# A two-layer hybrid decoder on one NeuronCore: late squares of the FFN norm, three attention stages, alternating GLA heads, 72 decay rows, another ending and a shorter warm-up

## The chip, the core and the metric

The kernel runs on one core of a Trainium2 chip. The metric is the device time of one execution, in microseconds (us); lower is better. The engines are TensorE (PE, with its weight loads shown apart as PEld), VectorE (DVE), ScalarE (ACT), GpSimd (POOL) and SyncE (SP, which issues most transfers). Each takes its instructions in the order in which they are in its queue.

## What is computed

Two layers over 512 positions of 1024 features, in float32. Each layer normalises x, makes one input projection, and gives its columns to four mixers: FoX (softmax attention with a cumulative log forget gate), GLA (gated linear attention in chunks of 64), MLA (attention over low-rank latents with a rotary part) and Mamba-2 SSD (with a convolution). Their outputs go through one output projection, and then come a second norm and a SwiGLU FFN. Cut to the frame:

```python
for l in range(DEPTH):
    h = rmsnorm(x, norm1[l])
    (fq, fk, fv, ff, gq, gk, gv, gr, gg, mcq, mckv, mkr, sz, sxbc, sdt) = split_cols(h @ w_in[l], IN_SPLITS)
    y_a = fox_mixer(fq, fk, fv, ff, fox_f_bias[l])
    y_b = gla_mixer(gq, gk, gv, gr, gg, gla_gate_w2[l], gla_gate_b[l], gla_out_norm[l])
    y_c = mla_mixer(mcq, mckv, mkr, positions, mla_q_norm[l], mla_w_uq[l], mla_kv_norm[l], mla_w_ukv[l])
    y_d = mamba2_mixer(sz, sxbc, sdt, ...)
    x = x + jnp.concatenate([y_a, y_b, y_c, y_d], axis=-1) @ w_out[l]
    h2 = rmsnorm(x, norm2[l])
    x = x + (jax.nn.silu(h2 @ w_gate[l]) * (h2 @ w_up[l])) @ w_down[l]
return rmsnorm(x, final_norm)
```

The four attention heads of FoX and of MLA are 64 wide; each query block has 128 positions and sees the keys up to its own block.

## The kernel before

x is held transposed: eight chunks `xT[0..7]` of 128 features by 512 positions. Each float32 operand of a large product is split in a high half (fp32r, made on ACT) and a low half (the rest, made on DVE), for weights (`wh`, `wl`, L293 and L294) and for activations. A product (`prod`, L315 to L317) is three matmuls for each chunk of 128 features: high by high, high by the weight's low half, and the activation's low half by high. Weights come by DMA from SP two ahead of their use, and only ACT and DVE stand between the transfer and the product.

The order of the instructions of PE, DVE and ACT is planned when the program is built, from the order of the code and the dependences; `tc.issue_after(x)` holds what follows in the code behind instruction x. The mixers are generators: `R.step()`, called after each product of the projections, takes the running ones a step on, so that their small pieces of work lie between the products.

The FFN norm is `norm2`. After each product of the last part of the output projection (tile `om`) the sum with x is made on DVE (L1072), `chunk` makes the chunk's high and low half with the norm's gain (`n_0h` on ACT, L363; `n_0l` on DVE, L364), and `square` squares the chunk on ACT (L371, L374) and adds it to the accumulator `n_0acc` on POOL, the last one on DVE (L375). The factor of the root is applied later, to the products. `first_two` (L396 to L407) computes the first columns of gate and up, `g` and `u`, over the first KC-1 = 7 of the 8 chunks, g then u, and then over the last chunk, and behind that sums the accumulator over the features (`n_0ms`, L407). In layer 1 the same tiles are called `n_1h`, `n_1l` and so on.

The decays of the SSD heads are a tile `jrr` of 40 rows by 512: rows 0 to 7 hold the high halves, rows 32 to 39 the low halves. The matmul `pb` (L526) picks one head's row with the matrix `sel` and spreads it over 128 partitions; there are four per layer. GLA adds the part from earlier chunks in groups of 14 matmuls (L671), two groups per layer, each for two heads: 7 chunks of one head, then 7 of the other. One matmul of float32 leaves two records in the trace. The two heads read other rows (32 each) and write other partitions (64 each) of one accumulator.

Attention (L682 to L735) works on 8 blocks (two pairs of heads, four query blocks). `front` makes the scores of one head (`sf` or `sm`, L692), mask and maximum on DVE, exponential and scaling on ACT. `back` turns the weights around on PE (`ptf` or `ptm`, L709), copies them on ACT (`atf` or `atm`, L711) and multiplies by v on PE (`fo` or `mo`, L714). The loop calls `front` for block j and then `back` for block j-1.

The end is `last_part`: the last products add to xT, and `xg` and the squares follow. Its last two chunks, 6 and 7, are computed in halves of the positions by `part(i, half, ...)`. `finish(half)` transposes `xg` (L777), sums the squares over partitions (`fms`, L805), scales and writes `foo` to the output (L814). In the second half all 16 transposes stand in `finish`. At the start, WARM matmuls of ones (`pps`, L195) run while x and the first weights come.

Of the kernel before, what the change touches and what calls it, by code (L numbers as in the profile page):

```python
# [17 lines left out]
ALU = mybir.AluOpType  # L18
# [22 lines left out]
RATE_F, RATE_M, RATE_S, RATE_G = 2, 2, 1, 2  # L41
WARM = 14
ROPE_AT = 3
# [92 lines left out]
def trunk(tc, I, out, shapes, depth=2):  # L136
# [7 lines left out]
    with ExitStack() as es:  # L144
# [74 lines left out]

        sel = cp.tile([40, 4, P], F32R, name="sel")  # L220

        def selectors():
            for half in range(2):
                V.tensor_copy(gmask[blk(half, 64)], tri[blk(half, 64), blk(half, 64)])
            for h in range(4):
                V.tensor_tensor(sel[:, h, :], ident[0:40, 4 + h:5 + h].broadcast_to((40, P)),
                                ident[0:40, 36 + h:37 + h].broadcast_to((40, P)), op=ALU.add)

# [123 lines left out]
        class Norm:  # L352


            def __init__(self, g0, name):
                self.g0, self.name, self.act = g0, name, []
# [39 lines left out]
            def first_two(self, pa_, pb_, split=KC - 1, with_col=True):  # L396

                wa, wb = W.get(), W.get()
                for ks in (range(split), range(split, KC)):
                    for ps, w in ((pa_, wa), (pb_, wb)):  # L400
                        last = prod(ps, w, self.act, ks=ks)
                with tc.issue_after(last.ins):
                    if with_col:
                        self.columns()
                        return self.spread()
                    ps = ps_mix(f"{self.name}ms")
                    PE.matmul(ps, lhsT=ones, rhs=self.acc, start=True, stop=True)  # L407
                    return rsqrt(ps, D, "f", self.name, sp.tile([P, T], F32, tag="rn", name=f"{self.name}r"))
# [13 lines left out]
        def joint_gates(l, sm, res):  # L422
# [161 lines left out]
        def gla(l, q, k, v, rg, Gc, res):  # L584
# [58 lines left out]
            for pr in range(2):  # L643
# [39 lines left out]
        def attention(l, nm, terms, v, res):  # L683
# [17 lines left out]

            def back(p, qb, ss, o):
                for k0 in range(0, qb + 1, 2):
# [7 lines left out]
                    S.copy(t[:, :n], pt[:, :n])  # L711
                    for kb in kbs:
                        for hh in range(2):
                            PE.matmul(o[blk(hh, 64), blk(qb)], lhsT=v[kb // 2][:, blk(4 * (kb % 2) + 2 * p + hh, 64)],  # L714
                                      rhs=t[:, blk(2 * (kb - k0) + hh)], start=kb == 0, stop=kb == qb)

            blocks = [(p, qb) for p in range(2) for qb in range(NB)]
            o, held = None, []
            for j in range(len(blocks) + 1):
                if j < len(blocks):  # L720
                    p, qb = blocks[j]
                    while len(terms) <= 2 * p + 1:
                        yield
                    held.append([])
                    for hh in range(2):
                        if hh:
                            yield
                        held[-1].append(front(2 * p + hh, qb))
                if j:
                    p, qb = blocks[j - 1]  # L730
                    if qb == 0:
                        o = ps_acc(f"{nm}o{l}_{p}")
                    back(p, qb, held.pop(0), o)
                    if qb == NB - 1:
                        res.append(mix_operand(o, f"{nm}{l}_{p}"))  # L735
                yield
# [23 lines left out]
        def last_part(us):  # L760


            acc, xg, banks = tmp("g", "nfacc"), [], {}

            def feature(m, ps, t):
                V.tensor_tensor(xT[m][:, t], xT[m][:, t], ps[:, t], op=ALU.add)
                V.tensor_scalar(xg[m][:, t], xT[m][:, t], col(104 + m), None, op0=ALU.mult)
                sq = tmp("f", f"nfq{m}") if m else acc
# [29 lines left out]
            def finish(half):  # L798
                bs = range(2 * half, 2 * half + 2)
                for m in range(KC) if half else (6, 7):  # L800
                    for b in bs:
                        turn(b, m, ps_proj if m >= 4 else ps_mix)
                ps = ps_mix(f"fms{half}")
                for b in bs:
                    PE.matmul(ps[:, b % 2:b % 2 + 1], lhsT=acc[:, blk(b)], rhs=onec, start=True, stop=True)  # L805
                rc = rsqrt_col(ps[:, 0:2], f"nf{half}", 2)
                for h in range(2):
                    for b in bs:
# [3 lines left out]
                        else:  # L812
                            S.activation(o, banks[b, h], AF.Copy, scale=rc[:, b % 2:b % 2 + 1])
                        nc.sync.dma_start(out[0, blk(b), blk(h, T)], o)  # L814

# [72 lines left out]
        for l in range(depth):  # L888
# [80 lines left out]
            for c in range(2):  # L969
                hold = {}  # L970
                for nm, scale, one, row in (("k", 1.0, -1.0, 66), ("q", -0.125, 1.0, 64)):
                    ps = ps_proj(f"f{nm}p{l}_{c}")
                    prod(ps, W.get(), act)
                    for hh in range(2):
# [9 lines left out]
                        G.memset(b.bitcast(F32)[64:68], one)  # L984
                        nc.gpsimd.dma_start(b[row:row + 2], rr[h:h + 33:32])
                        hold[nm, hh] = a, b
# [76 lines left out]
            for nm, ops in (("g", mix_g), ("m", mix_m)):  # L1063
                if nm == "m":
                    R.drain(g_m)
                for i in range(2):
                    w = W.get()
                    for c in range(4):
# [71 lines left out]
```

## Time and profile before

| | before |
|---|---|
| median of 3 runs | 1269.92 us (1268.7 to 1270.27) |
| profiled execution | 1269.87 us |
| its span, first to last instruction | 1268.1 us |
| mean granted TensorE clock | 0.994 |
| PE busy | 1248.9 us, 98% of the span |
| DVE, ACT, POOL busy | 694.0, 533.5, 179.1 us |

The profile is of one execution, and the span leaves out 1.77 us of its time. Busy time is summed over the instructions of an engine; a matmul's shown length is longer than its step, as matmuls are pipelined, so steps are read from start to start. A granted clock of 1.00 is 2.4 GHz for TensorE and 0.50 is 1.2 GHz.

### The profile page before, as it was taken

Reading aid. Unit: us, or ns where it says so; the run is one execution under the profiler, and the core shown is the slowest. Engines: PE = TensorE matmul, PEld = TensorE weight load, DVE = VectorE, ACT = ScalarE, POOL = GpSimd, SP = SyncE. Lnnn points to the kernel's source line nnn. Section 1 sums busy time; section 2 is a strip of 40 time slices with the busy share of each in tenths; the row PEclk is TensorE's granted clock in tenths of the full one; section 3 lists DMA queues with packets and bytes.
Section 4 is the critical chain, followed back from the end, with each engine's and each line's share of the span. In section 5 each row is a group of like instructions: output and inputs, shape, how many; then the busy total and the mean of one; then the engine's idle time right before and its main releaser. Section 6 shows DMA issues by size and latency. Waiting matters only on the chain.

```text
span 1268.1 us, 16210 instructions
## 1 busy us (share of the span) xinstructions
PE 1248.9 (98%) x6402; PEld 1014.5 (80%) x6402; DVE 694.0 (55%) x1132; ACT 533.5 (42%) x882; POOL 179.1 (14%) x163
## 2 busy tenths in 40 slices
PE   9999999989999999999999999999899999999997
PEld 7887787768888888888888877777788888888886
DVE  7877697565443333344557677966644334433444
ACT  6557765543222222223444577565422222212232
POOL 0103210031100110111301122000211011101111
PEclk9999999989999999999999999999999999999999
DMA  6222121113333333332323221212233223333232
GB/s 206 89 84 67 58 68 45 47 60 116 90 95 99 100 94 91 103 96 89 110 83 101 84 67 43 67 34 67 68 116 97 89 96 100 89 109 98 88 89 76
DMA packets 32907, 109.99 MB, mean 87 GB/s; under 512 B 4096, under 2 KB 4256, under 8 KB 32832
## 3 DMA queue, kind: packets, MB, share of 16 engines
q1 hardware_dynamic: 31968, 108.54, 27.7%
q8 instruction: 50, 0.82, 0.3%
q10 hardware_dynamic: 288, 0.34, 0.1%
q14 instruction: 25, 0.20, 0.0%
q0 software_dynamic: 576, 0.08, 0.0%
HBM read 106.79 MB, written 2.10 MB: 86 GB/s over the span
## 4 chain that ended last, share of the span: by engine, by line
PE 92%; DVE 5%; ACT 2%; DMA 1%; issue 0%; POOL 0%; SPq 0%; DVEq 0%
PE u L315 6%; PE u L316 6%; PE u L317 6%; PE g L317 6%; PE g L315 6%; PE g L316 6%; PE d L315 5%; PE d L316 5%; PE d L317 5%; PE ft L317 3%; PE ft L316 3%; PE ft L315 3%; PE sm L692 1%; PE oa L316 1%; PE oa L315 1%; PE oa L317 1%
## 5 line engine op out<-in xcount | busy, mean ns | idle before, releaser
L293 ACT CAST wh<-wr 128x1024 fp32r<-128x1024 f32 (+2 forms) x206 | 210.3, 1023 | 567.1 <-issue 342.5
L294 DVE TENSOR_TENSOR wl<-wr,wh 128x1024 fp32r<-128x1024 f32 (+2 forms) x206 | 249.9, 1213 | 73.2 <-ACT wh L293 73.0
L315 PE MATMUL d<-uh,wh 128*128 128x512 f32 x296 | 115.1, 389 | 0.0
L316 PE MATMUL d<-uh,wl 128*128 128x512 f32 x296 | 115.1, 389 | 0.0
L317 PE MATMUL d<-ul,wh 128*128 128x512 f32 x296 | 115.1, 389 | 0.0
L1097 DVE TENSOR_TENSOR ft<-u,fs 128x512 f32<-128x512 f32 x44 | 30.4, 692 | 132.7 <-PE u L317 127.1
L1111 DVE TENSOR_TENSOR xT<-xT,d 128x512 f32<-128x512 f32 x40 | 27.5, 688 | 104.6 <-PE d L317 104.6
L1094 POOL TENSOR_TENSOR fs<-fs,n_0r 128x512 f32<-128x512 f32 x22 | 38.3, 1744 | 280.4 <-ACT fs L1093 280.4
L1094 POOL TENSOR_TENSOR fs<-fs,n_1r 128x512 f32<-128x512 f32 x22 | 38.3, 1745 | 279.3 <-ACT fs L1093 279.3
L317 PE MATMUL g<-n_1l,wh 128*128 128x512 f32 x176 | 69.0, 392 | 2.3 <-DVE n_1l L364 2.3
L317 PE MATMUL g<-n_0l,wh 128*128 128x512 f32 x176 | 69.0, 392 | 2.3 <-DVE n_0l L364 2.3
L315 PE MATMUL g<-n_0h,wh 128*128 128x512 f32 x176 | 69.0, 392 | 0.8 <-ACT n_0h L363 0.8
L315 PE MATMUL g<-n_1h,wh 128*128 128x512 f32 x176 | 69.0, 392 | 0.8 <-ACT n_1h L363 0.8
L315 PE MATMUL u<-n_0h,wh 128*128 128x512 f32 x176 | 69.5, 395 | 0.0
L316 PE MATMUL u<-n_0h,wl 128*128 128x512 f32 x176 | 69.4, 394 | 0.0
L317 PE MATMUL u<-n_0l,wh 128*128 128x512 f32 x176 | 69.4, 394 | 0.0
L315 PE MATMUL u<-n_1h,wh 128*128 128x512 f32 x176 | 69.0, 392 | 0.0
L317 PE MATMUL u<-n_1l,wh 128*128 128x512 f32 x176 | 69.0, 392 | 0.0
L316 PE MATMUL u<-n_1h,wl 128*128 128x512 f32 x176 | 68.9, 392 | 0.0
L316 PE MATMUL g<-n_0h,wl 128*128 128x512 f32 x176 | 68.5, 389 | 0.0
L316 PE MATMUL g<-n_1h,wl 128*128 128x512 f32 x176 | 68.5, 389 | 0.0
L317 PEld LDWEIGHTS d<-ul,wh 128*128 128x128 f32 x296 | 55.6, 188 | 11.6
(614 smaller groups left out, 2823.5 us busy)
## 6 DMA issues: line engine op xcount, KB each, us to landing
wr<-in_weights_dram SPq DMA_DIRECT2D x168, 512.0 KB, 3.5
wr<-in_weights_dram SPq DMA_DIRECT2D x32, 448.0 KB, 3.2
xT<-in_x_dram SPq DMA_DIRECT2D x8, 256.0 KB, 6.8
out_dram<-foo SPq DMA_DIRECT2D x8, 256.0 KB, 2.4
wr<-in_weights_dram SPq DMA_DIRECT2D x6, 256.0 KB, 4.1
posi<-in_positions_dram ACTq DMA_DIRECT2D x1, 256.0 KB, 3.0
fkb<-jrr POOLq DMA_DIRECT2D x8, 4.0 KB, 2.7
fqb<-jrr POOLq DMA_DIRECT2D x8, 4.0 KB, 1.7
```

Source lines behind the costliest of these rows:

```text
L293: S.copy(h[:, c], raw[:, c])
L294: V.tensor_tensor(lo[:, c], raw[:, c], h.bitcast(F32)[:, c], op=ALU.subtract)
L315: PE.matmul(ps, lhsT=wh[:, k, c0:c0 + P], rhs=ah, start=k == 0, stop=False)
L316: PE.matmul(ps, lhsT=wl[:, k, c0:c0 + P], rhs=ah, start=False, stop=False)
L317: last = PE.matmul(ps, lhsT=wh[:, k, c0:c0 + P], rhs=al, start=False, stop=k == n - 1)
L692: PE.matmul(ps[:, :n], lhsT=q[:d, blk(qb)], rhs=k[:d, :n], start=i == 0, stop=i == len(terms[h]) - 1)
L1094: G.tensor_tensor(s, s, r, op=ALU.mult)
L1097: V.tensor_tensor(t, pu, s, op=ALU.mult)
L1111: V.tensor_tensor(xT[m], xT[m], ps, op=ALU.add)
```

## The change

1. `norm2`: no `square` between the chunks; `first_two` puts all squares and their sum behind the last chunk's halves, all adds on DVE, and its split is 6 and 2 chunks instead of 7 and 1.
2. `jrr` and `sel` have 72 rows; the low halves lie in rows 64 to 71.
3. GLA's loop over chunks is outside, that over the two heads inside.
4. Attention: `back` is split in `turn` (transposes and copies) and `values` (products by v). In step j come the values of block j-2, the scores of block j, and the transposes of block j-1.
5. Ending: the squares of chunk 7 are not added on DVE, but summed over partitions by matmuls of their own into the same place; eight transposes of the second half stand ahead of that half's last products; the second half's other transposes take buffers of another pool; the output's last piece is issued by ACT.
6. WARM is 11 instead of 14.

The core of the diff:

```diff
-WARM = 14
+WARM = 11
...
-        sel = cp.tile([40, 4, P], F32R, name="sel")
+        sel = cp.tile([72, 4, P], F32R, name="sel")
...
-                V.scalar_tensor_tensor(al, src, g, ah.bitcast(F32), op0=ALU.mult, op1=ALU.subtract)
+                low = V.scalar_tensor_tensor(al, src, g, ah.bitcast(F32), op0=ALU.mult, op1=ALU.subtract)
                 self.act.append((ah, al))
-                return high
+                self.last = high, low
...
                 for ks in (range(split), range(split, KC)):
                     for ps, w in ((pa_, wa), (pb_, wb)):
                         last = prod(ps, w, self.act, ks=ks)
+                if self.acc is None:
+                    high, low = self.last
+                    with tc.issue_after(high.ins), tc.issue_after(low.ins):
+                        for k in range(KC):
+                            self.square(k, V)
...
-            rr = sp.tile([40, T], F32R, tag="jrr", name=f"jrr{l}")
+            rr = sp.tile([72, T], F32R, tag="jrr", name=f"jrr{l}")
             G.memset(rr.bitcast(F32), 0.0)
             V.tensor_copy(rr[0:8], rows)
-            V.tensor_tensor(rr[32:40], rows, rr.bitcast(F32)[0:8], op=ALU.subtract)
+            V.tensor_tensor(rr[64:72], rows, rr.bitcast(F32)[0:8], op=ALU.subtract)
...
-                for hh in range(2):
-                    h = 2 * pr + hh
-                    for c in range(1, 8):
+                for c in range(1, 8):
+                    for hh in range(2):
+                        h = 2 * pr + hh
                         PE.matmul(o[blk(hh, 64), blk(c, 64)], lhsT=st[c][blk(h, 32), :],
...
-            for j in range(len(blocks) + 1):
+            for j in range(len(blocks) + 2):
+                if j < len(blocks):
+                    while len(terms) <= 2 * blocks[j][0] + 1:
+                        yield
+                if j >= 2:
+                    p, qb = blocks[j - 2]
+                    if qb == 0:
+                        o = ps_acc(f"{nm}o{l}_{p}")
+                    values(p, qb, turned.pop(0), o)
+                    if qb == NB - 1:
+                        res.append(mix_operand(o, f"{nm}{l}_{p}"))
                 if j < len(blocks):
...
+                    held.append([front(2 * p, qb)])
+                    yield
+                    held[-1].append(front(2 * p + 1, qb))
+                if 0 < j <= len(blocks):
+                    turned.append(turn(*blocks[j - 1], held.pop(0)))
                 yield
...
-                if m:
+                if m == KC - 1:
+                    end[t.start] = sq
+                elif m:
...
-                for m in range(KC) if half else (6, 7):
+                for m in range(4, KC) if half else (6, 7):
...
                 for b in bs:
-                    PE.matmul(ps[:, b % 2:b % 2 + 1], lhsT=acc[:, blk(b)], rhs=onec, start=True, stop=True)
+                    for sq in (acc, end[256 * half]):
+                        PE.matmul(ps[:, b % 2:b % 2 + 1], lhsT=sq[:, blk(b)], rhs=onec, start=sq is acc,
+                                  stop=sq is not acc)
...
-            part(0, 1, range(SECOND_HALF, n))
+            last = part(0, 1, range(SECOND_HALF, n))
+            with tc.issue_after(last.ins):
+                for m in range(4):
+                    for b in (2, 3):
+                        turn(b, m, ps_mix)
             part(1, 1, range(n))
...
                         if nm == "m":
                             norm2.chunk(m)
-                            norm2.square(m)
...
-                        r = norm2.first_two(pg, pu, with_col=False)
+                        r = norm2.first_two(pg, pu, KC - 2, with_col=False)
```

How the change moves instructions, at three places. A row is a line of the code, the operation, and the tiles that it writes and reads.

The first is DVE at the end of the output projection of layer 0, where `xT` is the residual add, `wl` a weight's low half, `n_0l` a chunk's low half. Before:

```order
L364 SCALAR_TENSOR_TENSOR n_0l_2727<-xT_86,pcv,n_0h_2726 128x512
L1072 TENSOR_TENSOR xT_88<-xT_88,om_5_2754 128x512
L294 TENSOR_TENSOR wl_2736<-wr_2733,wh_2735 128x1024
L364 SCALAR_TENSOR_TENSOR n_0l_2748<-xT_87,pcv,n_0h_2747 128x512
L364 SCALAR_TENSOR_TENSOR n_0l_2763<-xT_88,pcv,n_0h_2762 128x512
L1072 TENSOR_TENSOR xT_89<-xT_89,om_6_2769 128x512
L1072 TENSOR_TENSOR xT_90<-xT_90,om_7_2784 128x512
L294 TENSOR_TENSOR wl_2804<-wr_2801,wh_2803 128x1024
L364 SCALAR_TENSOR_TENSOR n_0l_2778<-xT_89,pcv,n_0h_2777 128x512
L364 SCALAR_TENSOR_TENSOR n_0l_2793<-xT_90,pcv,n_0h_2792 128x512
L375 TENSOR_TENSOR n_0acc<-n_0acc,n_0q_2796 128x512
```

Now:

```order
L1094 TENSOR_TENSOR xT_88<-xT_88,om_5_2737 128x512
L1094 TENSOR_TENSOR xT_89<-xT_89,om_6_2749 128x512
L364 SCALAR_TENSOR_TENSOR n_0l_2734<-xT_87,pcv,n_0h_2733 128x512
L364 SCALAR_TENSOR_TENSOR n_0l_2746<-xT_88,pcv,n_0h_2745 128x512
L1094 TENSOR_TENSOR xT_90<-xT_90,om_7_2761 128x512
L364 SCALAR_TENSOR_TENSOR n_0l_2758<-xT_89,pcv,n_0h_2757 128x512
L294 TENSOR_TENSOR wl_2778<-wr_2775,wh_2777 128x1024
L364 SCALAR_TENSOR_TENSOR n_0l_2770<-xT_90,pcv,n_0h_2769 128x512
L375 TENSOR_TENSOR n_0acc<-n_0acc,n_0q_2837 128x512
L375 TENSOR_TENSOR n_0acc<-n_0acc,n_0q_2840 128x512
L375 TENSOR_TENSOR n_0acc<-n_0acc,n_0q_2843 128x512
L375 TENSOR_TENSOR n_0acc<-n_0acc,n_0q_2846 128x512
```

Six more adds into `n_0acc` stand on DVE behind the last low half (seven in all), and none stands on POOL; the last weight split ahead of the FFN has moved back by one low half.

The second is PE in FoX of layer 0, around the transposes of block (1, 2). Before, with `gvp` a product of the input projection and `fo` the values:

```order
L709 MATMUL ptf_1_2_0_1744<-ident,asf_2_2_1623 128x128
L709 MATMUL ptf_1_2_0_1744<-ident,asf_3_2_1632 128x128
L709 MATMUL ptf_1_2_0_1744<-ident,asf_2_2_1623 128x128
L709 MATMUL ptf_1_2_0_1744<-ident,asf_3_2_1632 128x128
L709 MATMUL ptf_1_2_2_1755<-ident,asf_2_2_1623 128x128
L709 MATMUL ptf_1_2_2_1755<-ident,asf_3_2_1632 128x128
L324 MATMUL gvp_2_1772<-wh_1521,n_0h_154 128x256
L325 MATMUL gvp_2_1772<-wl_1522,n_0h_154 128x256
L326 MATMUL gvp_2_1772<-wh_1521,n_0l_155 128x256
L324 MATMUL gvp_2_1772<-wh_1521,n_0h_165 128x256
L714 MATMUL fo_1_1569<-atf_1_2_0_1749,fv_0_895 64x128 x4
L714 MATMUL fo_1_1569<-atf_1_2_2_1758,fv_1_896 64x128 x2
```

Now:

```order
L326 MATMUL gvp_1_1693<-wh_1584,n_0l_234 128x256
L726 MATMUL fo_1_1614<-atf_1_1_0_1640,fv_0_892 64x128 x4
L698 MATMUL sf_2_3_1723<-fka_2_1074,fqa_2_1160 128x512
L698 MATMUL sf_2_3_1723<-fkb_2_1075,fqb_2_1161 128x512
L698 MATMUL sf_3_3_1732<-fka_3_1083,fqa_3_1169 128x512
L698 MATMUL sf_3_3_1732<-fkb_3_1084,fqb_3_1170 128x512
L717 MATMUL ptf_1_2_0_1741<-ident,asf_2_2_1620 128x128
L717 MATMUL ptf_1_2_0_1741<-ident,asf_3_2_1629 128x128
L717 MATMUL ptf_1_2_0_1741<-ident,asf_2_2_1620 128x128
L717 MATMUL ptf_1_2_0_1741<-ident,asf_3_2_1629 128x128
L717 MATMUL ptf_1_2_2_1748<-ident,asf_2_2_1620 128x128
L717 MATMUL ptf_1_2_2_1748<-ident,asf_3_2_1629 128x128
```

The values behind these transposes, four products after them before, come a step later; those of the block ahead stand in front of the scores `sf`.

The third is PE at the end, behind the last product. Before (8 more transposes ahead of these rows):

```order
L777 MATMUL fo_1_10168<-ident,xg_9946 128x128
L777 MATMUL fo_1_10166<-ident,xg_9984 128x128
L777 MATMUL fo_1_10168<-ident,xg_9984 128x128
L777 MATMUL fo_1_10166<-ident,xg_10020 128x128
L777 MATMUL fo_1_10168<-ident,xg_10020 128x128
L777 MATMUL fo_1_10166<-ident,xg_10022 128x128
L777 MATMUL fo_1_10168<-ident,xg_10022 128x128
L805 MATMUL fms_10176<-ones,nfacc 128x1 x2
```

Now, behind the last product, and then behind the last product of chunk 6's second half:

```order
L793 MATMUL fo_1_10163<-ident,xg_9943 128x128
L793 MATMUL fo_1_10165<-ident,xg_9943 128x128
L793 MATMUL fo_1_10163<-ident,xg_9981 128x128
L793 MATMUL fo_1_10165<-ident,xg_9981 128x128
L793 MATMUL fo_1_10163<-ident,xg_10017 128x128
L793 MATMUL fo_1_10165<-ident,xg_10017 128x128
L822 MATMUL fms_10173<-ones,nfacc 128x1
L793 MATMUL fo_1_10163<-ident,xg_10019 128x128
L793 MATMUL fo_1_10165<-ident,xg_10019 128x128
L822 MATMUL fms_10173<-ones,nfq_256_10161 128x1
L822 MATMUL fms_10173<-ones,nfacc 128x1
L822 MATMUL fms_10173<-ones,nfq_256_10161 128x1
```

```order
L316 MATMUL dl_10018<-uh_21_9793,wl_9948 128x256
L317 MATMUL dl_10018<-ul_21_9794,wh_9947 128x256
L793 MATMUL fo_0_10128<-ident,xg_9799 128x128
L793 MATMUL fo_0_10130<-ident,xg_9799 128x128
L793 MATMUL fo_0_10128<-ident,xg_9835 128x128
L793 MATMUL fo_0_10130<-ident,xg_9835 128x128
L793 MATMUL fo_0_10128<-ident,xg_9871 128x128
```

Eight transposes have moved ahead of the last 21 products, and the sum over partitions is made by four matmuls, two of which read the squares of chunk 7, `nfq_256`.

## Rows read from the trace of the kernel before

**Rows 1.** The page: the start of the chain that ended last, shares of the span.
```profile
PE 92%; DVE 5%; ACT 2%; DMA 1%; issue 0%; POOL 0%; SPq 0%; DVEq 0%
```

**Rows 2.** Two stretches: us, busy of PE, PEld, DVE, ACT, POOL; granted clock; DMA.
```profile
256.00:268.00 12.00, 12.00 (x54) 9.94 (x53) 11.59 (x14) 9.57 (x15) 6.83 (x5) 1.00 0.17 50
...
276.00:280.00 4.00, 4.00 (x11) 3.10 (x10) 0.00 (x0) 0.00 (x0) 0.00 (x0) 0.50 0.00 0
```

**Rows 3.** Timeline, PE, FFN start of both layers: start, us, what [idle before].
```profile
265.74 0.39 PE L315 MATMUL g<-n_0h,wh 128*128 128x512 f32 x1
...
269.36 0.39 PE L316 MATMUL g<-n_0h,wl 128*128 128x512 f32 x1
...
274.16 0.79 PE L317 MATMUL g<-n_0l,wh 128*128 128x512 f32 x1 [1.92 <-DVE n_0l L364]
...
283.34 1.02 PE L407 MATMUL n_0ms<-n_0acc,ones 128*128 128x512 f32 x2
...
889.47 0.39 PE L315 MATMUL g<-n_1h,wh 128*128 128x512 f32 x1
...
905.92 1.02 PE L407 MATMUL n_1ms<-n_1acc,ones 128*128 128x512 f32 x2
```

**Rows 4.** Tiles n_0l, n_0q (ns min/median/max) and timeline, DVE and POOL.
```profile
L364 DVE SCALAR_TENSOR_TENSOR n_0l<-xT,pcv,n_0h x16: 736/752/1779, 5.3 to 274.0; 128x512 fp32r<-128x512 f32 x16
...
266.63 3.48 DVE L364 SCALAR_TENSOR_TENSOR n_0l<-xT,pcv,n_0h 128x512 fp32r<-128x512 f32 x2
...
260.86 8.69 POOL L375 TENSOR_TENSOR n_0acc<-n_0acc,n_0q 128x512 f32<-128x512 f32 x5 [44.79 <-ACT n_0q L374]
...
L374 ACT ACTIVATE n_0q<-xT x14: 613/618/625, 16.5 to 272.5; 128x512 f32<-128x512 f32 x14
L375 DVE TENSOR_TENSOR n_0acc<-n_0acc,n_0q x8: 676/692/695, 17.4 to 274.7; 128x512 f32<-128x512 f32 x8
```

**Rows 5.** Timeline, PE, around one decay product and one 68-row score product.
```profile
98.42 0.28 PE L325 MATMUL fvp<-wl,n_0h 128*128 128x256 f32 x1
98.54 0.28 PE L326 MATMUL fvp<-wh,n_0l 128*128 128x256 f32 x1
98.75 0.50 PE L526 MATMUL pb<-jrr,sel 40*128 40x512 f32 x1
99.18 0.50 PE L315 MATMUL fkp<-n_0h,wh 128*128 128x512 f32 x1
99.52 0.40 PE L316 MATMUL fkp<-n_0h,wl 128*128 128x512 f32 x1
...
132.97 0.40 PE L692 MATMUL sf<-fkb,fqb 68*128 68x512 f32 x1
133.20 0.40 PE L692 MATMUL sf<-fka,fqa 128*128 128x512 f32 x1
```

**Rows 6.** PE, line 671: timeline of one group, then two stretches of it (records in brackets).
```profile
194.11 1.66 PE L671 MATMUL go<-gq,gst 32*64 32x64 f32 x28
...
195.00:195.30 0.30, 0.30 (x12) 1.00 0.00 0
...
195.30:195.60 0.30, 0.30 (x9) 1.00 0.00 0
```

**Rows 7.** Waits, PE: total us, times, longest, attention values.
```profile
PE fo L714 <- ACT atf L711: 2.6, 6, 0.9
```

**Rows 8.** Timeline, PE, start; and the chain that ended last in the same stretch.
```profile
1.14 6.13 PE L195 MATMUL pps<-ones 128*128 128x128 f32 x28 [1.14 <-DVE ones L187]
...
3.62 6.75 DMA xT<-in_x_dram
```

**Rows 9.** Timeline, end: PE, DVE and ACT after the last product.
```profile
1258.78 1.91 PE L777 MATMUL fo<-ident,xg 128*128 128x128 f32 x16
...
1259.49 0.42 ACT L769 ACTIVATE nfq<-xT 128x256 f32<-128x256 f32 x1 [1.39 <-DVE xT L766]
...
1260.53 0.50 PE L805 MATMUL fms<-ones,nfacc 128*128 128x1 f32 x4
```

More of the change, by code (lines that the diff above doesn't have):

```diff
@@ L225, in selectors @@
             for h in range(4):
-                V.tensor_tensor(sel[:, h, :], ident[0:40, 4 + h:5 + h].broadcast_to((40, P)),
-                                ident[0:40, 36 + h:37 + h].broadcast_to((40, P)), op=ALU.add)
+                V.tensor_tensor(sel[:, h, :], ident[0:72, 4 + h:5 + h].broadcast_to((72, P)),
+                                ident[0:72, 68 + h:69 + h].broadcast_to((72, P)), op=ALU.add)
         gsgn = cp.tile([P, 8], F32, name="gsgn")
@@ L355, in __init__ @@
             def __init__(self, g0, name):
-                self.g0, self.name, self.act = g0, name, []
+                self.g0, self.name, self.act, self.acc = g0, name, [], None
             def chunk(self, k, src=None):
@@ L700, in front, with turn @@
                 return s
-            def back(p, qb, ss, o):
+            def turn(p, qb, ss):
+                ts = []
                 for k0 in range(0, qb + 1, 2):
@@ L711, in back @@
                     S.copy(t[:, :n], pt[:, :n])
[L712 to L715, printed above, removed]
-            blocks = [(p, qb) for p in range(2) for qb in range(NB)]
-            o, held = None, []
-            for j in range(len(blocks) + 1):
+                    ts.append(t)
@@ new lines, in turn, with values @@
+                return ts
+            def values(p, qb, ts, o):
+                for kb in range(qb + 1):
+                    for hh in range(2):
+                        PE.matmul(o[blk(hh, 64), blk(qb)], lhsT=v[kb // 2][:, blk(4 * (kb % 2) + 2 * p + hh, 64)],
+                                  rhs=ts[kb // 2][:, blk(2 * (kb % 2) + hh)], start=kb == 0, stop=kb == qb)
+            blocks = [(p, qb) for p in range(2) for qb in range(NB)]
+            o, held, turned = None, [], []
+            for j in range(len(blocks) + 2):
[9 more added lines that the diff above has]
+                        res.append(mix_operand(o, f"{nm}{l}_{p}"))
@@ L720, in attention @@
                 if j < len(blocks):
                     p, qb = blocks[j]
[L722 to L735, printed above, removed]
+                    held.append([front(2 * p, qb)])
@@ L760, in last_part @@
         def last_part(us):
-            acc, xg, banks = tmp("g", "nfacc"), [], {}
+            acc, xg, banks, end = tmp("g", "nfacc"), [], {}, {}
             def feature(m, ps, t):
@@ L767, in feature @@
                 V.tensor_scalar(xg[m][:, t], xT[m][:, t], col(104 + m), None, op0=ALU.mult)
-                sq = tmp("f", f"nfq{m}") if m else acc
+                sq = tmp("f", f"nfq{m}_{t.start}") if m else acc
                 S.activation(sq[:, t], xT[m][:, t], AF.Square)
-                if m:
+                if m == KC - 1:
+                    end[t.start] = sq
+                elif m:
                     (G if m < KC - 2 else V).tensor_tensor(acc[:, t], acc[:, t], sq[:, t], op=ALU.add)
@@ L799, in finish @@
                 bs = range(2 * half, 2 * half + 2)
-                for m in range(KC) if half else (6, 7):
+                for m in range(4, KC) if half else (6, 7):
                     for b in bs:
-                        turn(b, m, ps_proj if m >= 4 else ps_mix)
+                        turn(b, m, ps_acc)
                 ps = ps_mix(f"fms{half}")
                 for b in bs:
-                    PE.matmul(ps[:, b % 2:b % 2 + 1], lhsT=acc[:, blk(b)], rhs=onec, start=True, stop=True)
+                    for sq in (acc, end[256 * half]):
+                        PE.matmul(ps[:, b % 2:b % 2 + 1], lhsT=sq[:, blk(b)], rhs=onec, start=sq is acc,
+                                  stop=sq is not acc)
                 rc = rsqrt_col(ps[:, 0:2], f"nf{half}", 2)
@@ L813, in finish @@
                             S.activation(o, banks[b, h], AF.Copy, scale=rc[:, b % 2:b % 2 + 1])
-                        nc.sync.dma_start(out[0, blk(b), blk(h, T)], o)
+                        (nc.scalar if (half, h, b) == (1, 1, 2) else nc.sync).dma_start(out[0, blk(b), blk(h, T)], o)
             n = len(us)
@@ L984, in trunk @@
                         G.memset(b.bitcast(F32)[64:68], one)
-                        nc.gpsimd.dma_start(b[row:row + 2], rr[h:h + 33:32])
+                        nc.gpsimd.dma_start(b[row:row + 2], rr[h:h + 65:64])
                         hold[nm, hh] = a, b
```

## The prediction

> **What bounds the kernel.** The first view is the page's chain of waits, followed back from the last instruction: 92% of it is TensorE (PE), 5% VectorE (DVE), 2% ScalarE (ACT) [rows 1]. So time is gained only where PE idles, runs at the lower clock, or spends more than a product's normal pitch on an instruction. The second view, a table of stretches, finds the large loss. From 256 to 268 us DVE is busy 11.59 of 12 us, and from 276 to 280 us PE is busy all the time at a granted clock of 0.50, its 1.2 GHz level [rows 2]. The timeline of that place shows the order of events: the FFN's products run evenly from 265.74, one waits 1.92 us for the low half `n_0l` at 274.16, and after these waits the clock is low until about 280 [rows 2, 3]. I then looked at single instructions whose pitch (start to next start) is above that of their kind, at PE's waits, and at both ends of the program [rows 5 to 9].
>
> The sum is made against the profiled execution, 1269.87 us (span 1268.1 and 1.77 around it), which is 0.05 below the median of the runs.
>
> **FFN norm.** The first two hidden columns are 48 products. Undisturbed they stand (269.36 - 265.74) / 16 = 0.226 us apart, 10.85 us in all. In layer 0 they take 283.34 - 265.74 = 17.60 us, in layer 1 905.92 - 889.47 = 16.45 [rows 3]. The losses are 6.75 and 5.60, together 12.35 us; they are both the waits and the products at the lower clock. What is late is DVE, which takes its instructions in order: a low half takes 0.75 us as a rule, but the two from 266.63 on take 3.48 together, while POOL is inside its five adds of squares from 260.86 to 269.55, 1.74 us each [rows 4]. The change takes all six POOL adds out, puts the squares and their sum behind the last low half on ACT and DVE, and holds back two chunks rather than one in both columns. The last low half starts at 274.0 now and would end near 274.8. The pair at 266.63 alone is 2.0 us over two at 0.75; the others behind chunk 1 are stretched too, up to 1.78 [rows 4], and I take 4.2 us for all, which puts the end at 270.6. With the new order it is the 42nd product that needs it, at 265.74 + 41 x 0.226 = 275.0; even with the 2.0 us of the pair alone (272.8) it is in time. So nothing waits there, and without a wait I expect no low clock. ACT's eight squares at 0.62 are 5.0 us behind the high halves, to about 275.5, and the last add of 0.69 ends near 276.2 [rows 4]; PE is through its 48 products at 265.74 + 10.85 = 276.6. The sum is ready 0.4 us before it is needed. That is narrow, but a miss of some tenths costs those tenths only. Term: **-12.3**. The other end: if the DVE adds take POOL's 1.74 us, seven of them after 271.2 end at 283.4, which is when the sum of squares is read now, and the gain is nothing.
>
> **72 decay rows.** A decay product on 40 rows is 99.18 - 98.75 = 0.43 us, where a score product of the same 512 columns on 68 rows is 0.23. The product before it has a pitch of 0.21 instead of 0.12, the one after it 0.34 instead of 0.23 [rows 5]. So its tile size, unlike its neighbours', costs 0.20 + 0.09 + 0.11 = 0.40. There are eight. With 72 rows it is a tile of the neighbours' size: 8 x 0.40 = **-3.1**, rounding down. Setting 72 rows to zero or copying the decay rows to partition 64 costs no more per instruction, as the length per row is unchanged; at the other end nothing is gained.
>
> **GLA heads alternate.** A group of 28 records lasts 1.66 us, 0.058 per record, the two heads one after the other [rows 6]. Around the place where the first head ends and the second begins, 12 records fall into 0.30 us; later, in the second head alone, 9 do [rows 6]. The records of two heads, which use other rows and other columns of the array, start in pairs there. With the heads alternating all can pair: 14 x 0.058 and about 0.14 for the two edges are 0.95, a saving of 0.64, and 4 x 0.64 = **-2.5**. The other end is 0. A rule speaks against this term: the Trainium skill (TensorEngine Tiling (Array Packing), Gotcha 1: PSUM Pressure) says that different row tiles cannot access one PSUM bank at the same time. Both heads write one bank, so by that rule the term would be 0. The 12 records against 9 in the same bank speak against the rule.
>
> **Attention in three stages.** A block's scores (front), the transposes of its weights (turn) and its product with v (values) were two pieces, the values right behind the transposes, or a few products behind. Now the values stand one step later, ahead of the next scores. PE waited 2.6 us in six places for the copy `atf` that the values read [rows 7]; a step of products now lies between, and I take all of it. Further, values and scores stand side by side, so products change their kind less often; counted over PE's order that is 15 switches fewer each way. A switch shows 0.09 to 0.11 around a decay product [rows 5]; 15 x 0.1 less what two split groups in the out-projection cost is 1.0. Term: **-3.6**, between -6 (if the shorter waits of weight loads count as well) and +1.6 (the six waits stay, six more of their mean, 0.43, come at the new place, and only the 1.0 is gained).
>
> **Shorter warm-up.** 28 records in 6.13 us become 22, so the first product could start some 1.3 us earlier. But behind it the chain of waits goes back to the transfer of x, from 3.62 to 10.37 [rows 8]. Cover is that transfer; **0**, from -0.3 to +1.5 (if the products before it ran at the lower level of the clock, half the pace, for 3 us more).
>
> **The end.** Two instructions per half become four sums over partitions, and each is two records of 0.12 (four in 0.50) [rows 9]. In the first half these four more records lie on the path: +0.45. Eight of the last sixteen transposes, (1260.53 - 1258.78) / 16 = 0.109 each [rows 9], go ahead of the last part's products. They do not vanish; they move those products by 0.87, and one more change of kind adds 0.09. Behind the last product there were 16 transposes and 4 records, 2.2 us. Now 6 transposes run while ACT's last square comes, 1259.49 + 0.42 - 1258.78 = 1.13 after the transposes began [rows 9]; two transposes and six records behind it end some 1.85 after, 0.35 sooner. The last output's issue from ACT beside SP may give 0.1. Sum 0.45 + 0.96 - 0.35 - 0.1: **+1.0**, between -1.3 (the eight transposes and DVE's dropped add of 0.42 count in full) and +1.4.
>
> **Sum.** -12.3 - 3.1 - 2.5 - 3.6 + 0 + 1.0 = -20.5, so 1269.87 - 20.5 = **1249.4 us**.
>
> **Rivals.**
> 1. *The sum of squares is late.* ACT's eight squares, DVE's seven adds and PE's reading of them lie within 0.4 us. If they come 3 us late in each layer, PE idles before `n_0ms`, and the clock may fall behind that wait as it does now. Half of the FFN term goes: 1255.5. For it: DVE is full up to the last low half. Against it: POOL no longer works beside it.
> 2. *GLA gains nothing*, because records of two heads that write the same bank follow each other as those of one head do: 1249.4 + 2.5 = 1251.9. Against it stand the 12 records in 0.30 us. This is how the kernel would go by the Trainium skill's page TensorEngine Tiling (Array Packing), Gotcha 1.
> 3. *The squares do not do what they are moved for.* If low halves are slow for another reason than POOL's adds, the waits and the low clock stay: 1249.4 + 12.3 = 1261.7. Against it: the lows are at 0.75 wherever POOL is idle.
> 4. *Slower: the values block the scores.* PE takes its instructions in order, and the values now stand in front of the next scores in each of 32 steps (two layers, two attentions, eight blocks). If ACT's copy is late there, the scores wait as well, then DVE and ACT behind them, and the next copy is late again. The longest present wait of this kind is 0.9 us [rows 7]; at every step it would be 28.8 us, and 1278. The kernel is slower than before from 20.5 / 32 = 0.64 us a step on. Against it: a step of products lies between copy and use.
>
> **Chances.** Forecast 0.63; sum late 0.14; GLA nothing 0.12; squares without effect 0.07; slower 0.04. A measurement of this kernel can tell some 0.2%, 2.5 us, from no change. Only rival 4 is above that, and the cases between are few: faster 0.94, same 0.02, slower 0.04. The low end takes attention at -6 and the end at -0.3, less what may fail elsewhere: 1245. The high end holds rivals 1 and 2, and both together by half: 1257.5. Rivals 3 and 4 and a worse rival 1 lie outside, under 0.2.
>
> **What would show it.** Right: the 48 products last about 10.9 us in both layers, no stretch of PE shows a granted clock below 1.00 there, and low halves take 0.75. Decay products have a pitch of 0.23. A GLA group lasts about 1.0 us. Waits of the values for `atf` are gone. The end from the last product to the end of the span is shorter by about 0.4, but the products before it end later. Wrong: a wait of PE ahead of `n_0ms`, a granted clock of 0.50 behind it, GLA groups still at 1.6, or waits of the values in every step.

## The result, and the profile after

The changed kernel takes 1249.18 us (median of 4 runs, 1248.92 to 1250.93), the kernel before 1269.31 on the same chip; the ratio is 0.9845, with a 95% interval of 0.9828 to 0.9862. The forecast was 1249.4. The profiled execution is 1249.44 us, its span 1247.7, so the spans differ by 20.4 us. Cut at the same products in both traces, the difference lies here (first product of the ninth column `sm`: 19.31 before, 19.01 after; the other cuts are the rows below and [rows 3]):

| stretch | forecast | measured |
|---|---|---|
| start, to `sm` | 0 | -0.3 |
| mixers of layer 0, to the first `g` | -4.6 | 241.9 against 246.4: -4.5 |
| FFN start, layer 0 (48 products) | -6.75 | 10.89 against 17.60: -6.7 |
| from there to the first `g` of layer 1 | -4.6 | 601.7 against 606.1: -4.4 |
| FFN start, layer 1 | -5.60 | 10.88 against 16.45: -5.6 |
| the rest, with the end | +1.0 | 363.3 against 362.2: +1.1 |

The page's chain of waits is now 96% PE, 92% before [rows 1]:

```profile
PE 96%; DVE 2%; DMA 0%; issue 0%; ACT 0%; SPq 0%; DVEq 0%
```

The stretches at the FFN's start (us, busy time of PE, PEld, DVE, ACT and POOL with instructions, granted clock, DMA): no POOL work up to 276, and the clock at 1.00, where [rows 2] has 0.50.

```profile
256.00:268.00 12.00, 12.00 (x55) 9.93 (x54) 11.69 (x18) 9.47 (x16) 0.00 (x0) 1.00 0.30 101
268.00:272.00 4.00, 4.00 (x19) 3.34 (x18) 2.81 (x5) 1.06 (x1) 0.00 (x0) 1.00 0.00 0
272.00:276.00 4.00, 4.00 (x17) 2.96 (x17) 3.04 (x4) 3.29 (x5) 0.00 (x0) 1.00 0.42 132
276.00:280.00 4.00, 4.00 (x20) 3.30 (x19) 2.55 (x5) 2.50 (x4) 1.44 (x2) 1.00 0.43 130
```

PE's timeline there, the first product and the sum of squares in each layer: 48 products at 0.227 us, without a wait in between, answering to [rows 3].

```profile
260.95 0.39 PE L315 MATMUL g<-n_0h,wh 128*128 128x512 f32 x1
...
271.84 1.02 PE L413 MATMUL n_0ms<-n_0acc,ones 128*128 128x512 f32 x2
...
873.54 0.39 PE L315 MATMUL g<-n_1h,wh 128*128 128x512 f32 x1
...
884.42 1.02 PE L413 MATMUL n_1ms<-n_1acc,ones 128*128 128x512 f32 x2
```

DVE and ACT, answering to [rows 4]: the last low half takes 0.75, and behind it come seven adds in 5.47 us; ACT's seven further squares take 3.74 and end at 267.97. So DVE's adds end last: the sum is ready at 270.88 and is read at 271.84, 0.96 us later.

```profile
264.75 0.75 DVE L364 SCALAR_TENSOR_TENSOR n_0l<-xT,pcv,n_0h 128x512 fp32r<-128x512 f32 x1
265.41 5.47 DVE L375 TENSOR_TENSOR n_0acc<-n_0acc,n_0q 128x512 f32<-128x512 f32 x7
...
264.23 3.74 ACT L374 ACTIVATE n_0q<-xT 128x512 f32<-128x512 f32 x7
```

PE around the decay product that answers to [rows 5]: pitches 0.11, 0.23 and 0.24, where 0.21, 0.43 and 0.34 stood.

```profile
97.83 0.28 PE L326 MATMUL fvp<-wh,n_0l 128*128 128x256 f32 x1
97.94 0.39 PE L532 MATMUL pb<-jrr,sel 72*128 72x512 f32 x1
98.17 0.39 PE L315 MATMUL fkp<-n_0h,wh 128*128 128x512 f32 x1
98.41 0.40 PE L316 MATMUL fkp<-n_0h,wl 128*128 128x512 f32 x1
```

A GLA group and the product behind it: 28 records in 0.96 us from start to next start, 1.59 before [rows 6].

```profile
190.14 1.03 PE L677 MATMUL go<-gq,gst 32*64 32x64 f32 x28
191.10 0.50 PE L316 MATMUL oa<-f_0mh,wl 128*128 128x512 f32 x1
```

All waits of PE in the list (us in total, times, longest). Those for `n_0l`, `n_0h` and `atf` [rows 7] are gone. New are three small ones: `ga` for `gks` in GLA, and two of the input projection (`ft`) for weights.

```profile
PE pps L195 <- DVE ones L187: 1.1, 1, 1.1
PE uv L324 <- DVE mkh L1049: 0.8, 2, 0.4
PE gs L639 <- DVE gst L643: 0.8, 2, 0.4
PE ft L315 <- ACT wh L293: 0.6, 1, 0.6
PE ga L658 <- DVE gks L631: 0.5, 2, 0.2
PE ft L316 <- DVE wl L294: 0.2, 1, 0.2
```

The end, behind the last product, answering to [rows 9]: six transposes, two more after the last `xg`, and then the last sums. `nf1v` starts 2.11 us behind the first transpose; it was 2.29 before (first row here, against the first of [rows 9]).

```profile
1261.07 0.16 DVE L344 TENSOR_SCALAR nf1v<-fms 128x2 f32<-128x2 f32 x1 [0.70 <-PE fms L805]
...
1238.61 0.82 PE L793 MATMUL fo<-ident,xg 128*128 128x128 f32 x6
...
1239.68 0.44 PE L793 MATMUL fo<-ident,xg 128*128 128x128 f32 x2
...
1240.32 0.36 PE L822 MATMUL fms<-ones,nfq 128*128 128x1 f32 x2
1240.72 0.16 DVE L344 TENSOR_SCALAR nf1v<-fms 128x2 f32<-128x2 f32 x1 [1.10 <-PE fms L822]
```

### The profile page after: what moved, and what is told of

Read it like the earlier page. It is cut to its first block, busy times and chain, and to the rows that moved or that the text cites. A ratio compares the mean times of both kernels' runs of the same rounds, so it can differ in the third digit from the quotient of the medians.

```text
span 1247.7 us, 16211 instructions
## 1 busy us (share of the span) xinstructions
PE 1236.5 (99%) x6404; PEld 1010.1 (81%) x6404; DVE 691.6 (55%) x1142; ACT 533.5 (43%) x882; POOL 159.8 (13%) x151
## 4 chain that ended last, share of the span: by engine, by line
PE 96%; DVE 2%; DMA 0%; issue 0%; ACT 0%; SPq 0%; DVEq 0%
PE g L316 6%; PE u L316 6%; PE g L317 6%; PE u L317 6%; PE g L315 6%; PE u L315 6%; PE d L317 5%; PE d L316 5%; PE d L315 5%; PE ft L316 3%; PE ft L317 3%; PE ft L315 3%; PE sm L698 2%; PE sf L698 1%; PE dl L315 1%; PE dl L317 1%
## 5 line engine op out<-in xcount | busy, mean ns | idle before, releaser
L316 PEld LDWEIGHTS d<-uh,wl 128*128 128x128 f32 x296 | 55.6, 188 | 11.6
```

The costliest lines, as they stand in the source:

```text
L316: PE.matmul(ps, lhsT=wl[:, k, c0:c0 + P], rhs=ah, start=False, stop=False)
```

## The experiments

**1. The FFN part alone.** The kernel before with the late squares, the adds on DVE and the split.

```diff
+                if self.acc is None:
+                    ...
+                            self.square(k, V)
...
-                            norm2.square(m)
...
-                        r = norm2.first_two(pg, pu, with_col=False)
+                        r = norm2.first_two(pg, pu, KC - 2, with_col=False)
```

> The kernel before with part 1 of the change alone (late squares, all adds on VectorE, split of 6 and 2 chunks). Theory: the losses of 6.7 and 5.6 us at the FFN's start go, so the span falls by 12.2 (11.8 to 12.6) to about 1255.9, and the 48 products last 10.9 us in both layers. Rival (the parts need each other, the FFN's start is only free because the mixers before it are shorter): a part of the loss stays, the 48 products last over 12 us, and the gain is under 10.

Measured: 1256.88 us (4 runs), ratio 0.9902 (0.9886 to 0.9919); span 1255.3. The 48 products last 276.21 - 265.33 = 10.88 in layer 0 and 10.89 in layer 1. The gain at the two places is 6.7 and 5.6 us, with nothing of the other parts in the kernel: the term stands by itself.

**2. No POOL adds.** The kernel before with its early squares, but without six of the seven adds of each FFN norm, so that its sum lacks the squares of chunks 1 to 6.

```diff
-                            norm2.square(m)
+                            if m in (0, KC - 1):
+                                norm2.square(m)
+                            else:
+                                S.activation(tmp("f", f"n2_{l}q{m}"), xT[m], AF.Square)
```

> The kernel before with early squares on ScalarE as they were, but without the six adds on GpSimd in each FFN norm; it leaves the squares of chunks 1 to 6 out of that norm's sum. Theory (GpSimd's adds slow VectorE's low halves): the low halves take 0.75 us at the FFN's start, the last one ends near 270.6, and the 48 products last under 12 us with the granted clock at 1.00: span about 1256 to 1258. Rival (the order is at fault: residual adds 6 and 7 and a weight split stand ahead of the last two low halves, and the squares stand between the high halves): low halves are at 0.75, but the products still wait and last 14 us or more.

Measured: span 1255.2, the 48 products 276.05 - 265.17 = 10.88. The low halves of both norms of layer 0 (ns min/median/max), then two stretches with columns as above:

```profile
L364 DVE SCALAR_TENSOR_TENSOR n_0l<-xT,pcv,n_0h x16: 734/748/754, 5.4 to 269.0; 128x512 fp32r<-128x512 f32 x16
...
268.00:272.00 4.00, 4.00 (x20) 3.30 (x19) 2.32 (x4) 1.07 (x2) 0.00 (x0) 1.00 0.44 135
272.00:276.00 4.00, 4.00 (x19) 3.34 (x18) 0.00 (x0) 0.43 (x1) 0.00 (x0) 1.00 0.00 0
```

The longest low half is 754 ns, 1779 in [rows 4], though nothing but POOL's adds is missing. So POOL's adds were the whole cause. The early squares on ACT, the order on DVE and the old split are as in the kernel before, and cost nothing here.

**3. Late adds on POOL.** The changed kernel with `self.square(k)` for `self.square(k, V)`.

> The changed kernel with the six late adds of each FFN norm back on GpSimd. Theory: no low half is slowed, as the adds come behind the last of them, but six adds of 1.3 to 1.7 us, one after the other from about 265, end at 273 to 275, and the sum is read 1.8 to 4.1 us later in each layer: span 1251 to 1257, more if the clock falls behind the wait. Rival (all that matters is that the low halves are in time): no wait ahead of the sum, span as changed, 1247.7.

Measured: span 1252.7, 5.0 more than changed. PE's waits, POOL's adds, and two stretches:

```profile
PE n_0ms L413 <- DVE n_0acc L375: 2.2, 1, 2.2
PE n_1ms L413 <- DVE n_1acc L375: 2.2, 1, 2.2
...
264.84 8.54 POOL L375 TENSOR_TENSOR n_0acc<-n_0acc,n_0q 128x512 f32<-128x512 f32 x6 [53.76 <-ACT n_0q L374]
...
272.00:276.00 4.00, 1.84 (x6) 1.23 (x7) 2.50 (x4) 1.00 (x1) 1.30 (x2) 1.00 0.00 0
276.00:280.00 4.00, 4.00 (x19) 3.27 (x19) 2.98 (x5) 1.90 (x3) 0.00 (x0) 1.00 0.76 217
```

The six adds end at 273.4, PE waits 2.2 us ahead of the sum in each layer, and each layer is 2.5 us longer. The granted clock stays at 1.00 behind this one wait. That speaks against the second half of my first rival: the low clock of before came with three waits (0.41, 0.85 and 1.92 us, between 269.75 and 274.16), a single one of 2.2 did not bring it. A sum that is 3 us late, as the rival has it, was not run.

**4. Early adds on DVE.** The changed kernel with `norm2.square(m, V)` between the chunks.

> The changed kernel with the squares early again, between the chunks, but all adds on VectorE. Theory: six adds of 0.69 between the low halves delay the last low half by 4.1 us, from 265.5 to 269.6, still ahead of the 42nd product at 270.2: the 48 products last 10.9 to 11.5 us, span 1247.5 to 1249. Rival (the early place itself costs, whichever engine adds): waits for low halves and a granted clock below 1.00, span over 1255.

Measured: span 1249.5. The 48 products last 10.88 us in layer 0 and 10.89 in layer 1, so the place of the squares doesn't matter as long as POOL isn't used; the last low half ends at 270.97 and is needed at 262.75 + 41 x 0.227 = 272.0. Of the 1.8 us over the changed kernel 1.74 are in the start: `sm` comes at 20.75 instead of 19.01. The row of the last low half, and PE in three stretches of the start (us, busy PE with records, granted clock, DMA):

```profile
270.23 0.74 DVE L364 SCALAR_TENSOR_TENSOR n_0l<-xT,pcv,n_0h 128x512 fp32r<-128x512 f32 x1
...
7.00:9.00 2.00, 0.85 (x3) 1.00 1.00 381
9.00:11.00 2.00, 1.98 (x6) 0.62 1.05 400
11.00:13.00 2.00, 2.00 (x6) 0.52 0.98 285
```

The expected span was missed by a cause that the theory had not in view; experiments 9, 10 and 12 are on it.

**5 to 7. One part alone, on the kernel before.** 72 rows (`sel`, `jrr` as in the change); GLA's loops exchanged; the three attention stages.

> The kernel before with 72 decay rows alone. Theory: each of the eight decay products has the tile size of its neighbours, its pitch falls from 0.43 to 0.23 (to 0.33 where a product of another kind stands beside it) and the products around it lose their 0.09 and 0.11: span 2.3 to 3.2 us less, 1265 to 1265.8. Rival (the pitch is the matmul's own, as its right side is another tensor): pitch stays at 0.43, span 1268.

> The kernel before with GLA's heads alternating alone. Theory: the records of two heads start in pairs in the same bank, a group takes 0.96 us instead of 1.59, four groups 2.5 us, span 1265.6. Rival (some of the gain comes from what the other parts leave around the groups): the group takes 0.96, but the waits ahead of what follows grow, span over 1266.5.

> The kernel before with the three attention stages alone. Theory: the 2.6 us of waits for the copies go, fewer changes of kind give some 1 us more, span 1264.0 to 1265.0. Rival (waits move to the new place): values wait at other places, span 1266 or more.

All three spans fell below what was expected of them. Single spans also carry differences of the start (`sm` between 18.73 and 19.37 in them) and of the FFN's start, which is unchanged in these kernels but took 16.5 to 16.6 us in five of its six places and 17.6 in one. So I read each part from the two stretches of the mixers, as in the table above:

| part | layer 0 | layer 1 | sum | forecast |
|---|---|---|---|---|
| 72 rows (span 1264.0) | -1.4 | -1.3 | -2.7 | -3.1 |
| GLA (span 1265.2) | -1.0 | -0.9 | -1.9 | -2.5 |
| three stages (span 1262.7) | -2.4 | -2.4 | -4.8 | -3.6 |
| sum | -4.8 | -4.6 | -9.4 | -9.2 |

With 72 rows, four of the eight decay products have a pitch of 0.23. The other four, behind the SSD's score matmuls, have 0.31, but there the matmul ahead has 0.03 where it had 0.20. Counted with their neighbours, six of the eight give 0.39 to 0.43 each. The third of each layer gives only some 0.1: the second head's scores behind it now come late, 0.28 after the first head's where it was 0.12, and their weight load had waited for DVE. PE's rows there, and the wait in the view of L692:

```profile
113.33 0.28 PE L692 MATMUL sf<-fkb,fqb 68*128 68x256 f32 x1
113.61 0.39 PE L692 MATMUL sf<-fka,fqa 128*128 128x256 f32 x1
...
  DVE sn_0v L332: 0.2, 1
```

In GLA each group takes 0.96 us as forecast, which is 0.63 less, but the second group's scores now wait, in the list of PE's waits:

```profile
PE ga L652 <- DVE gks L625: 0.5, 2, 0.2
```

The product ahead of that wait has a pitch of 0.62 instead of 0.32: 0.3 us per layer come back there. With three stages the waits for `atf` leave the list, and no new ones of the values come. These waits had cost more than the list's 2.6. Read by pitch, the product ahead of the values takes 1.15 us at this place of the kernel before, where 0.21 is its pitch without a wait:

```profile
169.01 0.28 PE L324 MATMUL gvp<-wh,n_0h 128*128 128x256 f32 x1
170.16 0.88 PE L714 MATMUL fo<-atf,fv 128*64 128x128 f32 x12 [0.87 <-ACT atf L711]
```

At four more places of the layer it took 0.64, 0.56, 0.48 and 0.39 where 0.32 is usual. That is 1.7 us per layer and 3.5 in both, an estimate from these pitches. With three stages no product ahead of the values stands above the usual pitch of its kind.

**8. The old ending.** The changed kernel with `last_part` of before.

> The changed kernel with the ending of before. Theory: the new ending costs 0.45 (four more records in the first half) and 0.96 (eight transposes ahead of the last products) and saves 0.35 and 0.1 behind them, so the old one is 1.0 to 1.1 us faster: span 1246.6, against 1247.7. Rival (the new ending gains what it was made for, and the 1.1 us between last product and span end came from elsewhere): the old ending is slower by 0.5 to 1.3 us.

Measured: 1248.2 us (1247.75 to 1250.07, 4 runs), ratio to before 0.9839 (0.9822 to 0.9855), span 1246.6. The two medians are 1.0 apart and their intervals overlap, so it is the traces that decide: up to the first `dl` (the first product of the last part) both kernels are alike (21.5 us ahead of before), at the span's end the changed one has lost 1.1 and this one nothing. Its end, as in [rows 9]:

```profile
1237.26 1.91 PE L791 MATMUL fo<-ident,xg 128*128 128x128 f32 x16
...
1239.01 0.51 PE L819 MATMUL fms<-ones,nfacc 128*128 128x1 f32 x4
1239.55 0.16 DVE L344 TENSOR_SCALAR nf1v<-fms 128x2 f32<-128x2 f32 x1 [0.70 <-PE fms L819]
```

**11. All transposes late.** The changed kernel without the eight early transposes.

```diff
-            last = part(0, 1, range(SECOND_HALF, n))
-            with tc.issue_after(last.ins):
-                for m in range(4):
-                    for b in (2, 3):
-                        turn(b, m, ps_mix)
+            part(0, 1, range(SECOND_HALF, n))
...
-                for m in range(4, KC) if half else (6, 7):
+                for m in range(KC) if half else (6, 7):
                     for b in bs:
-                        turn(b, m, ps_acc)
+                        turn(b, m, ps_acc if m >= 4 else ps_mix)
```

> The changed kernel with its eight moved transposes back behind the last product, the rest of the new ending kept. Theory: the last product comes 0.96 earlier, but 16 transposes and eight records behind it last 2.65 instead of 1.85: span 0.1 to 0.2 less, 1247.5. Rival (moving them early pays, as they fill a gap): span 1248 or more.

Measured: span 1247.6, and from the first `dl` on 0.2 us less than changed. So the move of the transposes costs 0.2 net. The rest of the 1.1 is the extra sums over partitions: from the first transpose to the first instruction behind the sums this kernel takes 0.45 us more than number 8, in each half.

**9, 10, 12. The start.** The changed kernel with the old ending and WARM = 14; the changed kernel with WARM = 8; and with the split 7 and 1, `KC - 1` for `KC - 2`.

> The changed kernel with the ending and the 14 warm-up matmuls of before. Theory: with 11 of them TensorE is idle for longer between warm-up and the second chunk, and in some executions the granted clock falls to 0.50 for about 4 us there, which costs 1.7 us (seen in one profile); with 14 it doesn't, and the usual time is the same as with 11, so all executions lie near 1247.8, none above 1249. Rival (the slow executions have another cause): about one in four stays at 1250.

> The changed kernel with 8 warm-up matmuls. Theory: the warm-up ends about 1.3 us earlier still while x and the second weights come no sooner, so the idle time grows and the low clock at the start comes in most executions: 1250.5 to 1251.5, the first product of the ninth column near 20.7 instead of 19.0. Rival (the end of the warm-up doesn't matter): 1249.0, as with 11.

> The changed kernel with the FFN's first two columns split 7 and 1 as before. Theory: the low halves are in time for this split too (the seventh at 264, needed at 265.4), so the 48 products last 10.9 us, and the span is as changed, 1247.7 (0.3 either way, unless the start falls to the low clock). Rival (the new split is a part of the gain): products wait for chunk 6, span 1249 or more with waits in both layers.

Number 12 answers its own question: 48 products in 10.89 and 10.88 us, so the split is no part of the gain. Its span is 1249.7 because `sm` comes at 21.00. PE in the same stretches as in experiment 4:

```profile
7.00:9.00 2.00, 0.56 (x2) 1.00 1.03 386
9.00:11.00 2.00, 1.77 (x5) 0.61 1.05 399
11.00:13.00 2.00, 2.00 (x6) 0.54 0.87 280
```

In the first of them PE is busy 0.56 of 2 us, as it waits 1.4 us for a weight; behind that the granted clock is near its lower level, and the products stand 0.427 us apart for some 3.5 us. Number 9 is 1248.29 us, all five executions between 1248.14 and 1248.75, ratio to before 0.9836 (0.9823 to 0.985). Among the six profiles with 11 warm-up matmuls, four have `sm` at 18.90 to 19.03 and two at 20.75 and 21.00; the seven with 14 have it between 18.73 and 19.37. With 11, one timed execution in four was 1.5 to 2.3 us above the others, in the changed kernel and in number 8. So the low clock at the start was seen with 11 alone, and 14 matmuls cost nothing in the usual execution. That 14 always keep the start even is not shown: five executions are few, and those of the kernel before, also with 14, can't tell, as they spread by 2.2 us and its FFN's start alone takes 16.5 or 17.6. The wait's length alone doesn't decide: 0.95 us (number 4) had the low clock behind it, 1.02 (number 11, also 11 matmuls) and 1.2 us with 14 (number 9) had not; what does was not tried further. With 8, number 10 takes 1251.29 (1250.47 to 1251.69), `sm` at 21.14. PE in the warm-up of number 10 and then of number 9 (records in brackets), then two later stretches of number 10, and its wait for weights:

```profile
4.00:5.00 1.00, 0.91 (x5) 1.00 0.80 263
...
4.20:5.20 1.00, 1.00 (x11) 1.00 0.72 257
...
9.00:11.00 2.00, 2.00 (x5) 1.00 1.04 397
11.00:13.00 2.00, 2.00 (x6) 1.00 0.84 244
...
PE ft L315 <- ACT wh L293: 1.5, 2, 0.9
```

Here too the products are 0.427 us apart up to 13 us, half pace, though the column of the granted clock reads 1.00. The forecast of the time holds, but its reason, a fall of the clock, is not what the trace shows. The warm-up's records stand 0.213 us apart to their end, where those of number 9 go over to 0.11 from 4.2 us on, and every product before 12.86 has a shown length of 0.63 us or more, where 0.39 to 0.40 is that of full pace. With 8 matmuls nothing ran at full pace before: the pace had not yet risen.

## Why the prediction was right

**FFN norm: right, place, cause and size.** 12.3 forecast, 12.3 measured. Experiment 2 shows the cause, POOL's adds beside DVE. The margin of the sum of squares, 0.4 us in the forecast, is 0.96, and its order was wrong: I had ACT's squares end last and one add behind them, and it is DVE's seven adds that do, 2.9 us behind the squares. Rival 3 falls with experiment 2, and rival 1 in its price: a sum that makes PE wait 2.2 us costs 2.5, with no fall of the clock (experiment 3). Of the change's three moves here (late squares, DVE, split) only the second is needed: experiments 4 and 12 each undo one of the others, and the 48 products stay at 10.9 us; both undone at once was not run. The exact agreement has some luck in it, as the loss at an unchanged FFN start differs from execution to execution: 5.6 to 5.7 us at five places of experiments 5 to 7, and 6.7 at the sixth.

**Mixers: right in the sum, by errors that cancel.** Attention was undersized, -4.8 for -3.6. The step that missed most is the 2.6 us taken for the waits: by the pitches they cost some 3.5, and 1.3 is left for "products change their kind less often", taken at 1.0 and tested by no run of its own. Rows and GLA were oversized by 0.4 and 0.6, both because the sum had no follower. Of "8 x 0.40" 0.27 comes back in each layer, where the scores behind the third decay product wait for DVE (`sn_0v`), and of "4 x 0.64" 0.3 in each layer, where `gks` on DVE is late next. The parts alone sum to -9.4, together they give -8.9. Of the 0.5 between, 0.4 lies at the fourth decay product of each layer: the values now stand right behind it, its pitch is 0.33 instead of 0.23, and it gives 0.2 instead of 0.39.

**GLA against the rule.** By the Trainium skill (TensorEngine Tiling (Array Packing), Gotcha 1: PSUM Pressure) different row tiles can't access the same PSUM bank at once. By that rule rival 2 would hold. The trace disagrees, for two heads that write other partitions of the bank: 28 records into one bank take 0.96 instead of 1.59 us.

**The end: right, +1.1 for +1.0**, though the split was another. The sums of the first half cost 0.45, as forecast. The transposes ahead of the last products were to cost 0.96, and the last product comes 0.85 later than in number 11. The stretch behind the last product was to be 0.35 shorter and is 0.18 shorter. The 0.1 for issuing the last output from ACT did not come: from the start of `nf1v` to the span's end it is 7.01 us before and after.

**The warm-up: 0 in the usual execution, as forecast; the upper bound of 1.5 was short.** Where the clock fell it cost 1.7 and 2.0 us (experiments 4 and 12).

**Rival 4** did not come: no wait of the values is in the list of the changed kernel.

The fastest version that ran is the change with the old ending; with 14 warm-up matmuls as well (number 9) its executions lie closest together, 0.9 us below the changed kernel by the medians. By the medians numbers 8 and 9 are alike (1248.20 and 1248.29).

## What to carry to other kernels

When elementwise work on DVE takes twice its usual time, look at what POOL does in the same stretch, before moving anything else: here it was worth 12 of 20 us. Work moved to an earlier place on the engine that bounds the kernel is not hidden by that, and a second small matmul in place of an add elsewhere is paid on that engine. A warm-up is to be judged by its slowest executions, not by the median alone.

## What the runs showed that was not expected

POOL's adds more than double an instruction of DVE beside them, 1779 ns against 754 at most without them, while POOL's own adds take 1.42 us each alone (8.54 for six, experiment 3) and 1.74 beside DVE [rows 4]. Not every DVE instruction is slowed: inside the same five adds of POOL, three residual adds of 128x512, which read a product (`om`), kept 0.68 us. One of them, in the kernel before:

```profile
262.68 0.68 DVE L1072 TENSOR_TENSOR xT<-xT,om 128x512 f32<-128x512 f32 x1
```

Why these are spared no run tests. A single wait of PE of 2.2 us left the granted clock where it was. And the granted clock's column doesn't show all half pace: it reads 1.00 at the start of number 10.
